# RWKV-7 chunk steps on Trainium2: one source order for all five engines, a norm in four stages, outputs in two tiles

## The chip, the core and the metric

The kernel runs on one core of a Trainium2 chip. A core has a matrix engine (TensorE, in the profile PE, with its weight loads as PEld), three elementwise engines (VectorE or DVE, ScalarE or ACT, GpSimd or POOL) and SyncE (SP), which here only issues DMAs. Each engine takes its own instructions strictly in order; across engines they wait for one another on semaphores. The metric is the device time of one execution in microseconds (us), as the median of several runs.

## What is computed

A decoder of two layers over 512 positions of width 1024 in float32: a sparse attention mixer with an MLP, then an RWKV-7 mixer with an MLP, and a last norm. The change is in the RWKV-7 mixer alone. Its core is a recurrence over the positions, for 16 heads of 64:

```
def step(state, inp):
    r_t, w_t, k_t, v_t, kk_t, b_t = inp
    sa = jnp.einsum('bhvk,bhk->bhv', state, -kk_t)
    state = (state * w_t[:, :, None, :] + sa[..., None] * b_t[:, :, None, :]
             + v_t[..., None] * k_t[:, :, None, :])
    y = jnp.einsum('bhvk,bhk->bhv', state, r_t)
    return state, y
...
y = ((y - mean) * lax.rsqrt(var + LNX_EPS) * lnx_w.astype(f32).reshape(H, N)
     + lnx_b.astype(f32).reshape(H, N))
bonus = jnp.sum(rh * kh * r_k.astype(f32), axis=-1, keepdims=True) * vh
out = (y + bonus).reshape(B, L, D).astype(h.dtype) * g
return out @ w_o
```

Here g is a gate, `sigmoid(xg @ g1) @ g2`.

## The kernel before

The recurrence runs in 8 chunks of 64 positions (NCH). Within a chunk the dependence of position on position is a triangular system, solved with matrices made beforehand; from chunk to chunk a state of 64 x 64 for each head goes on. All of it is in `rwkv()`.

**Ahead of the steps.** The v projection ("V") is a dense matmul into all 8 PSUM banks; `vcopy` brings it to the tiles VT. `vmean` and `vload(n)` take a mean over each head out of it and write the result to the operand tile sv of chunk n (POOL). The triangular matrices of all chunks are inverted in `solve`, in two halves, f = 0 for chunks 0 to 3 and f = 1 for chunks 4 to 7: 30 pairs of DVE instructions each (a product into pr, an addition into tn), a memset, a copy, then DMAs that spread the result into the tiles Mt and T11. `invert` is a generator: `run(t)` draws steps of it until their estimated time is t or more; `HOLD` (1e9) between its parts ends any draw. `until(f)` draws until half f is done.

**Operands of a chunk.** `opl(n, j)`, two halves j, makes products of the chunk's keys on PE into a PSUM tile with tag d (there are two of those), and masks them on DVE into abd (or AL) and BL. `opt(n)` transposes keys into BL. `merge1(n)` and `merge2(n)` extend the inverse from 32 x 32 blocks to 64, with a copy sa between and copies into Mt behind; `acopy(n)` moves a part by eight DMAs.

**A step** of chunk n: `step_z` (PE) and its copies Zb; `step_u` (PE) and four copies into sv; `step_s` and `step_n` (PE), which end in the product of the new state on DVE, in sv of the next chunk; `step_r` and `step_y` (PE) give the output y of the chunk, copied on ACT. The next `step_z` needs the new state. Then `gnorm(n)`: square (ACT), sum over a head (DVE), Sqrt (ACT), a reciprocal square root refined in four small DVE instructions, the product with it (DVE), the product with lnw (POOL), the addition of the bonus bv (POOL); `turn(n)` transposes y on PE into yT. `out(f)` takes yT of four chunks, adds a bias and multiplies by the gate gT (the tile ot, DVE), and splits it into a high part oh (ACT) and a low part ol (DVE or POOL). `wo(f)` is the output projection of that half, eight blocks m of 24 matmuls; its weights come as wraw by DMA and are split in two by ACT (L93) and DVE (L101). gT comes from `g2`, eight blocks of four matmuls.

**What sets the order.** Outside a block marked `manual_schedule` a scheduler places each engine's instructions by priority. Before, only PE was in such a block, and only in the loop over the steps: PE's order there was the source's, three pieces of a step with pieces of operands, merges, g2 (`G2P`) and wo(0) (`WOP`) drawn in between by `fill()`. DVE, ACT, POOL and SP were placed by the scheduler.

Of the kernel before, what the change touches and what calls it, by code (L numbers as in the profile page):

```python
# [10 lines left out]
OP = mybir.AluOpType  # L11
# [754 lines left out]
def rwkv(c, x, ks, gi):  # L766
# [348 lines left out]
    def merge(n):  # L1115
        mt = Mt[n // 4][:, :, n % 4]
        t11 = T11[n // 4]
        with c.hp("merge"):
            sa = merge1(mt, t11, n)
        yield  # L1120
        with c.hp("merge"):
            merge2(mt, sa)
        yield

    def merge1(mt, t11, n):
# [9 lines left out]
    def merge2(mt, sa):  # L1135
# [57 lines left out]
    def opt(n):  # L1193
# [4 lines left out]
        for i in range(2):  # L1198
            cp(TE[i], BL[n][E2[1 - i], 1, :, 64:128], pt[E2[i], :, 1])
# [40 lines left out]
    @c.site("g2")  # L1240
    def g2m(m, ah, al, bh):
# [375 lines left out]
```

## Time and profile before

| | us |
|---|---|
| median of 3 runs (1373.76 to 1376.73) | 1375.86 |
| the profiled execution | 1374.03 |
| its span on the core | 1372.2 |
| start: V's end to z of step 1 | 816.6 to 855.5 |
| six step periods: z of step 1 to z of step 7 | 855.5 to 960.3 |
| tail: z of step 7 to the start of wo(1), about | 960.3 to 982.0 |

Times within the span count from its start. A step period is told from one z to the next. PEclk is the clock that was granted to PE: 1.00 is 2.4 GHz and 0.50 is 1.2 GHz. A row such as "[4.17 <-DVE tn L1026]" says that the engine had stood for 4.17 us, and that an instruction of DVE at line 1026 on the tile tn ended the wait.

### The profile page before, as it was taken

The numbers are of one execution on the slowest core, as the hardware profiler recorded it, in microseconds if no ns is written. First come the engines' busy times: TensorE is split into PE (matmuls) and PEld (weight loads), VectorE is DVE, ScalarE is ACT, GpSimd is POOL, SyncE is SP. The second block draws the span as 40 slices with busy tenths as digits, with TensorE's granted clock in tenths as the row PEclk, the third lists the DMA queues.
The fourth block names the chain that finished last, engine by engine and source line by source line (L and its number), as shares of the span: only waits on it lengthen the run. The fifth ranks groups of instructions, "written<-read, shape, count | busy, mean of one in ns | idle before, by whom it ended". The sixth has DMA issues, their size and how long they took to land.

```text
span 1372.2 us, 20054 instructions
## 1 busy us (share of the span) xinstructions
PE 1295.9 (94%) x8197; PEld 1065.6 (78%) x8197; DVE 800.8 (58%) x1429; ACT 593.6 (43%) x1005; POOL 171.3 (12%) x168
## 2 busy tenths in 40 slices
PE   7989899999999999999999896877999999999997
PEld 6767566888888888898578674667988888888887
DVE  5689974553431445339888888577865532245422
ACT  5545693343311434228776332655543421134421
POOL 0386750000000000000000011334220000000000
PEclk9999999999999999999999895989999999999998
DMA  7100013221323224303302414433532222322401
GB/s 287 62 31 32 1 69 117 100 93 62 123 92 123 80 74 153 123 32 123 123 31 53 128 52 98 74 95 132 185 105 80 92 92 94 122 92 83 162 1 62
DMA packets 68283, 128.04 MB, mean 93 GB/s; under 512 B 32864, under 2 KB 39648, under 8 KB 67424
## 3 DMA queue, kind: packets, MB, share of 16 engines
q1 hardware_dynamic: 65952, 124.53, 27.7%
q10 hardware_dynamic: 2240, 2.24, 0.5%
q8 instruction: 64, 1.05, 0.3%
q14 instruction: 27, 0.22, 0.0%
HBM read 115.74 MB, written 6.82 MB: 89 GB/s over the span
## 4 chain that ended last, share of the span: by engine, by line
PE 80%; DVE 12%; issue 3%; ACT 2%; POOL 2%; DMA 1%; SPq 0%; ACTq 0%; DVEq 0%; POOLq 0%
PE g L119 20%; PE g L120 20%; PE g L121 20%; PE g L628 2%; PE d L613 1%; DVE rot L411 1%; DVE w L101 1%; DVE L L587 1%; DVE pr L1025 1%; DVE tn L1026 1%; POOL kl L99 1%; DVE acc L497 1%; PE g L1308 1%; PE g L993 1%; PE g L1324 1%
## 5 line engine op out<-in xcount | busy, mean ns | idle before, releaser
L101 DVE TENSOR_TENSOR w<-wraw,w 128x1024 fp32r<-128x1024 f32 x189 | 232.8, 1255 | 109.4 <-ACT w L93 109.1
L93 ACT ACTIVATE w<-wraw 128x1024 fp32r<-128x1024 f32 x198 | 201.2, 1048 | 139.9 <-DMA wraw<-in_wblk 106.9
L119 PE MATMUL g<-sh,w 128*128 128x512 f32 (+1 forms) x608 | 216.5, 356 | 0.0
L120 PE MATMUL g<-sl,w 128*128 128x512 f32 (+1 forms) x608 | 216.1, 355 | 0.0
L121 PE MATMUL g<-sh,w 128*128 128x512 f32 (+1 forms) x608 | 216.1, 355 | 0.0
L120 PE MATMUL g<-al,w 128*128 128x512 f32 x512 | 200.0, 391 | 0.2 <-DVE al L257 0.2
L119 PE MATMUL g<-ah,w 128*128 128x512 f32 x512 | 200.1, 391 | 0.0
L121 PE MATMUL g<-ah,w 128*128 128x512 f32 x512 | 199.9, 390 | 0.0
L273 ACT ACTIVATE sh<-r 128x512 fp32r<-128x512 f32 x64 | 40.4, 631 | 227.2 <-DVE r L271 227.2
L119 PEld LDWEIGHTS g<-sh,w 128*128 128x128 f32 x608 | 114.9, 189 | 16.4
L121 PEld LDWEIGHTS g<-sh,w 128*128 128x128 f32 x608 | 114.9, 189 | 16.3
L120 PEld LDWEIGHTS g<-sl,w 128*128 128x128 f32 x608 | 114.9, 189 | 16.2
L119 PEld LDWEIGHTS g<-ah,w 128*128 128x128 f32 x512 | 96.5, 189 | 20.2
L120 PEld LDWEIGHTS g<-al,w 128*128 128x128 f32 x512 | 96.4, 188 | 20.4 <-DVE al L257 0.6
L121 PEld LDWEIGHTS g<-ah,w 128*128 128x128 f32 x512 | 96.5, 189 | 20.1
L271 DVE SCALAR_TENSOR_TENSOR r<-g,rstd 128x512 f32<-128x512 f32 x64 | 44.1, 691 | 97.0 <-PE g L121 84.6
L275 DVE TENSOR_TENSOR sl<-q,sh 128x512 fp32r<-128x512 f32 x64 | 44.4, 693 | 75.1 <-ACT q L274 75.1
L295 DVE TENSOR_TENSOR x<-g,x 128x512 f32<-128x512 f32 x26 | 18.0, 691 | 107.4 <-PE g L121 107.4
L179 ACT ACTIVATE sq<-x 128x256 f32<-128x256 f32 (+1 forms) x56 | 26.7, 499 | 105.1 <-DVE x L295 56.4
L922 POOL MEMSET seg<- 128x512 f32 x1 | 0.5, 528 | 487.2 <-DVE xl L101 487.2
L597 ACT ACTIVATE L<-L,st 128x256 f32<-128x256 f32 (+3 forms) x64 | 35.1, 553 | 14.0 <-DVE st L595 13.9
L274 ACT ACTIVATE q<-r 128x512 f32<-128x512 f32 x64 | 39.4, 615 | 0.0
(310 smaller groups left out, 2458.6 us busy)
## 6 DMA issues: line engine op xcount, KB each, us to landing
wraw<-in_wblk SPq DMA_DIRECT2D x98, 1024.0 KB, 4.8
wraw<-in_wblk SPq DMA_DIRECT2D x5, 512.0 KB, 5.6
x<-in_xT SPq DMA_DIRECT2D x8, 256.0 KB, 5.1
x<-in_xT SPq DMA_DIRECT2D x2, 1024.0 KB, 6.5
xs<-x SPq DMA_DIRECT2D x2, 1024.0 KB, 4.9
abd<-AR SPq DMA_DIRECT2D x64, 32.0 KB, 1.9
vb<-VT SPq DMA_DIRECT2D x16, 128.0 KB, 3.8
x<-xs SPq DMA_DIRECT2D x2, 1024.0 KB, 5.1
```

What stands on the lines that cost most here:

```text
L93: s.wsp = s.nc.scalar.activation(hi, r, AF.Copy)
L101: s.nc.vector.tensor_sub(out, a, b)
L119: s.nc.tensor.matmul(p, whi[:, kc, :], ahi, start=first and kc == 0, stop=False)
L120: s.nc.tensor.matmul(p, whi[:, kc, :], alo, start=False, stop=False)
L121: s.nc.tensor.matmul(p, wlo[:, kc, :], ahi, start=False, stop=last and kc == KC - 1)
L179: nc.scalar.activation(sq, xk, AF.Square)
L271: nc.vector.scalar_tensor_tensor(r, p, 0.0, rstd, op0=OP.max, op1=OP.mult)
L273: nc.scalar.activation(hi, r, AF.Square)
L274: nc.scalar.activation(q, r, AF.Square)
L275: nc.vector.tensor_sub(lo, q, hi.bitcast(F32))
L597: nc.scalar.activation(L[g][:, :n], L[g][:, :n], AF.Exp, bias=nmx[:, g:g + 1], scale=0.125, accum_out=sm[:, g:g + 1])
L628: nc.tensor.matmul(po[HF[e]], v[sc // 2][:, j:j + 64], st8[tb, pr, e][:, sc], start=sc == 0, stop=sc == tb)
```

## The change

One block now sets the order of PE, ACT, DVE, SP and POOL together, from the copies of V to the end of the last step, and the engines' instructions in it stand as the source has them. The source order is written out anew. All eight blocks of g2 stand ahead of the steps, and all eight blocks of wo(0) behind them (four stood within them). The norm is in four stages gA (square), gB (sum), gC (Sqrt) and gD (the rest), which tables place one to three steps behind their chunk. The outputs of four chunks share a tile (two tiles in all). The bonus is taken straight from VT by two POOL instructions on 64 partitions each, so the tiles VB and their 16 DMAs go, and `bo` is one DVE copy where it was four. The copies of merges are all ACT's, two of four having been DVE's. The memsets of bd and sv stand earlier. Weights for wo(0) are fetched from behind the loop on.

```
-    bo = c.tmp.tile([128, NCH, 8], F32, name="bo", tag="bo", bufs=1)
-    for b in range(2):
-        for s in range(2):
-            nc.vector.tensor_copy(bo[E2[b], s::2].rearrange("p n (a e) -> p n a e", e=2), pbo[E2[s], :, :, b])
+    bo = c.tmp.tile([128, 64], F32, name="bo", tag="bo", bufs=1)
+    nc.vector.tensor_copy(bo, pb[:, 0, :64])
...
-        for b in range(2):
-            nc.sync.dma_start(VB[n][E2[b]].rearrange("p (a j) -> p a j", a=4), v4[:, :, b])
...
+    def gD(n, eng=nc.gpsimd):
+        sq, st = gs.pop(n)
+        m, sd, y, u, o = (st[:, i] for i in range(5))
+        nc.vector.reciprocal(y, sd)
+        nc.vector.tensor_mul(u, m, y)
+        nc.vector.scalar_tensor_tensor(u, u, -0.5, y, op0=OP.mult, op1=OP.mult)
+        nc.vector.scalar_tensor_tensor(o, u, 1.5, y, op0=OP.add, op1=OP.mult)
+        y3 = g3(YY[n])
+        nc.vector.tensor_tensor(y3, y3, o[:, :, None].to_broadcast([128, 8, 64]), op=OP.mult)
+        bv = c.t("bv")
...
+        for b in range(2):
+            nc.gpsimd.tensor_tensor(bv[E2[b]].rearrange("p (a e i) -> p a e i", a=4, e=2), v4[:, :, b],
+                                    bs[:, :, b, :, None].to_broadcast([64, 4, 2, 64]), op=OP.mult)
         eng.tensor_tensor(y3, y3, lnw, op=OP.mult)
+        eng.tensor_tensor(YY[n], YY[n], bv, op=OP.add)
...
-    until(0)
+    with c.tc.manual_schedule(engines=set(MAN)):
+        run(9e8)
+        run(1)
+        run(1)
+        for i in VL[:3]:
+            vcopy(i)
+        vmean(0)
+        vload(0)
+        opn(1, 0)
+        for i in VL[3:]:
+            vcopy(i)
+        del ps
+        opn(1, 1)
...
+        g2(0)
+        g2(1)
+        opt(1, (0, 0))
+        g2(2)
+        g2(3)
+        step_z(0)
+        for m in range(4, 8):
+            g2(m)
+        vload(1)
+        run(RUN1)
+        merge2(0, merge1(0))
+        for n in range(NCH):
+            more = n < NCH - 1
+            if n:
+                step_z(n)
...
+            if n and more:
+                acopy(n + 1)
+                opn(n + 1, 0)
+                vload(n + 1)
+            for k in GB.get(n, ()):
+                gB(k)
+            if n < 3:
+                run(RUN2)
+            step_u(n)
+            if more and n != 3:
+                sa[n + 1] = merge1(n + 1)
+            for k in GB.get(n, ()):
+                gC(k)
+            if more:
+                pn = step_s(n)
+                step_n(n, pn)
+            py = step_r(n)
+            if more:
+                sbd(n)
+            step_y(n, py)
+            for k in GB.get(n, ()):
+                gD(k)
...
+            if n and more:
+                opn(n + 1, 1)
+            if n == 3:
+                sa[4] = merge1(4)
+            if more:
+                merge2(n + 1, sa[n + 1])
+            if n and n < NCH - 2:
+                opt(n + 1, (0, 0) if n < 3 else TE)
+            for k in TU.get(n, ()):
+                turn(k)
+            for k in GA.get(n, ()):
+                gA(k)
+    c.prefetch(PFA)
+    out(0)
+    gB(6)
+    gC(6)
+    gD(6)
+    gA(7)
...
+    gD(7, nc.vector)
     w0 = wo(0)
...
+    turn(5)
+    turn(6)
+    for _ in w0:
+        pass
+    turn(7)
     out(1)
...
+GA = {2: (0,), 3: (1, 2), 4: (3,), 5: (4,), 6: (5,), 7: (6,)}
+GB = {3: (0,), 4: (1, 2), 5: (3,), 6: (4,), 7: (5,)}
+TU = {4: (0,), 5: (1, 2), 6: (3,), 7: (4,)}
```

Three places show what that does to the engines' rows. The first is DVE after V. Lines 1025 and 1026 are the inverse (its first half has the tile tn_6101 before and tn_6098 in the change, its second half tn_6099 in the change); vm is the mean, and d, kon to abd and BL are the masks of chunk 1. Before:

```order
L1025 TENSOR_TENSOR pr_6139<-tn_6101 128x198
L1273 TENSOR_REDUCE vm_6442<-VT_6431 128x16
L1026 TENSOR_TENSOR tn_6101<-tn_6101,pr_6139 128x9x22
L1274 TENSOR_SCALAR vm_6442<-vm_6442 128x16
L1273 TENSOR_REDUCE vm_6442<-VT_6431 128x16
L1025 TENSOR_TENSOR pr_6139<-tn_6101 128x184
L1274 TENSOR_SCALAR vm_6442<-vm_6442 128x16
L1273 TENSOR_REDUCE vm_6442<-VT_6432 128x16
L1026 TENSOR_TENSOR tn_6101<-tn_6101,pr_6139 128x8x23
L1179 TENSOR_TENSOR abd_5987<-d_6459,kon_2262 64x4x64
L1025 TENSOR_TENSOR pr_6139<-tn_6101 128x168
L1179 TENSOR_TENSOR abd_5987<-d_6459,kon_2262 64x4x64
```

Now, the last rows of the second half and what follows (the 62 rows of that half stand together, right behind the last of the first half):

```order
L1026 TENSOR_TENSOR tn_6099<-tn_6099,pr_6401 128x2x29
L1025 TENSOR_TENSOR pr_6401<-tn_6099 128x30
L1026 TENSOR_TENSOR tn_6099<-tn_6099,pr_6401 128x30
L1028 MEMSET tn_6099 128x32
L1029 COPY tn_6099<-tn_6099 128x1024
L1245 TENSOR_REDUCE vm_6431<-VT_6428 128x16
L1246 TENSOR_SCALAR vm_6431<-vm_6431 128x16
L1171 TENSOR_TENSOR abd_5984<-d_6503,kon_2262 64x4x64
L1171 TENSOR_TENSOR BL_6502<-d_6503,kon_2262 128x4x64 x2
L1171 TENSOR_TENSOR abd_5984<-d_6529,kon_2262 64x4x64
L1171 TENSOR_TENSOR BL_6502<-d_6529,kon_2262 128x4x64 x2
L1290 TENSOR_TENSOR sv_6430<-g_6712,pc_5323 64x512
```

The mean and the masks stood among the first half's last rows; now both halves of the inverse are ahead of them. The second place is PE at the same point, from the last rows of opl(1) on. Before (L1244 to L1247 g2, L1196 opt, L1129 merge1, L1308 z):

```order
L1185 MATMUL d_6487<-AR_5061,KB_5867 64x64
L1244 MATMUL g_6444<-sg_5351,w_6340 128x512
...
L1244 MATMUL g_6480<-sg_5351,w_6340 128x512
L1196 MATMUL d_6508<-ident_75,KB_5360 128x128 x2
...
L1129 MATMUL g_6524<-T11_6367,Mt_5421 32x32
L1244 MATMUL g_6544<-sg_5351,w_6340 128x512
...
L1139 MATMUL g_6551<-Mt_5421,sa_6541 32x32
L1308 MATMUL g_6577<-sv_6441,abd_5987 64x64 x3
```

Now (L1176 opl, with d_6503 its first half and d_6529 its second; L1233 g2, L1188 opt, L1260 z, L1119 merge1):

```order
L1177 MATMUL d_6503<-AR_5059,KB_5526 64x64
L1176 MATMUL d_6529<-AR_5060,KB_5702 64x128 [waits DVE_49,PE_49]
...
L1233 MATMUL g_6551<-sg_5351,w_6337 128x512
...
L1188 MATMUL d_6565<-ident_75,KB_5360 128x128 x2
...
L1260 MATMUL g_6591<-sv_6430,abd_5984 64x64 x16
...
L1119 MATMUL g_6640<-T11_6364,Mt_5421 32x32 x8
```

The second half of opl(1) now waits for a DVE instruction, the last mask of the first half, whose PSUM tile it takes over; g2, opt and z stand behind it. The third place is behind the last step, on PE and POOL. PE before, around the end of step 7 (L1354 y, L1396 turn, w and oh or ol a block of wo(0)):

```order
L121 MATMUL g_8240<-oh_7854,w_7502 128x256
L1354 MATMUL g_8184<-sv_6441,BL_7921 64x64 x16
L1396 MATMUL g_8287<-ident_75,y_7834 128x128 x4
...
L119 MATMUL g_8353<-oh_7854,w_8155 128x256
L1396 MATMUL g_8401<-ident_75,y_8114 128x128 x4
```

PE now (L1310 y, L1363 turn of chunks 4, 5 and 6):

```order
L1310 MATMUL g_8021<-sv_6430,BL_7818 64x64 x16
L1363 MATMUL g_8058<-ident_75,y_7492 128x128 x4
L1363 MATMUL g_8147<-ident_75,y_7492 128x128 x4
L1363 MATMUL g_8153<-ident_75,y_7492 128x128 x4
L119 MATMUL g_8163<-oh_8084,w_8070 128x256
L120 MATMUL g_8163<-ol_8085,w_8070 128x256
```

wo(0) had begun ahead of y of step 7; now its first row is behind the turn of chunk 6. POOL's last rows of the mixer before (L1383 is the product with lnw, L1387 the addition of bv, L99 an ol):

```order
L99 TENSOR_TENSOR ol_7855<-ot_7876,oh_7854 128x256
L99 TENSOR_TENSOR ol_7855<-ot_7884,oh_7854 128x256
L1386 TENSOR_TENSOR bv_8040<-vb_7416,bo_5973 128x512
L1383 TENSOR_TENSOR y_7834<-y_7834,lnw_6520 128x512
L1387 TENSOR_TENSOR y_7834<-y_7834,bv_8040 128x512
L1386 TENSOR_TENSOR bv_8237<-vb_7645,bo_5973 128x512
```

And now (L1353 lnw, L1354 the addition, L1351 bv):

```order
L1353 TENSOR_TENSOR y_7492<-y_7492,lnw_6792 128x512
L99 TENSOR_TENSOR ol_8085<-ot_8090,oh_8084 128x256
L1351 TENSOR_TENSOR bv_8126<-VT_6429,bo_5973 64x512 x2
L99 TENSOR_TENSOR ol_8085<-ot_8098,oh_8084 128x256
L1354 TENSOR_TENSOR y_7492<-y_7492,bv_8126 128x512
L1351 TENSOR_TENSOR bv_8142<-VT_6429,bo_5973 64x512 x2
L99 TENSOR_TENSOR ol_8085<-ot_8106,oh_8084 128x256
L99 TENSOR_TENSOR ol_8085<-ot_8114,oh_8084 128x256
```

The four ol of POOL stood ahead of the norms of the last three chunks; now they stand among the operations of chunks 6 and 7.

## Rows read from the trace of the kernel before

**Rows 1.** The page: busy tenths and granted clock in 40 slices.

```profile
PE   7989899999999999999999896877999999999997
PEclk9999999999999999999999895989999999999998
```

**Rows 2.** Stretches: start:end length, busy PE, PEld, DVE, ACT, POOL, clock, DMA share.

```profile
834.20:855.50 21.30, 16.66 (x248) 13.76 (x250) 19.02 (x52) 6.01 (x13) 0.00 (x0) 0.50 0.49 100
...
884.30:898.10 13.80, 11.15 (x273) 9.36 (x274) 7.66 (x17) 9.00 (x19) 4.29 (x5) 1.00 0.13 21
898.10:913.90 15.80, 14.11 (x273) 12.16 (x273) 8.98 (x19) 7.08 (x15) 5.35 (x6) 0.78 0.52 134
...
855.50:960.30 104.80, 85.77 (x1716) 73.02 (x1712) 68.64 (x147) 59.61 (x118) 39.77 (x35) 0.92 0.39 99
...
870.80:873.00 2.20, 2.20 (x18) 1.54 (x12) 1.07 (x3) 0.37 (x1) 1.26 (x1) 1.00 0.23 37
954.40:960.30 5.90, 5.90 (x52) 5.77 (x50) 3.24 (x10) 4.49 (x8) 0.44 (x1) 1.00 0.54 181
```

**Rows 3.** Timeline of PE: start, length, engine, line, operation, [idle before <-releaser].

```profile
848.71 0.70 PE L1324 MATMUL g<-bd,Mt 128*64 128x128 f32 x4 [4.17 <-DVE tn L1026]
...
855.52 0.47 PE L1308 MATMUL g<-sv,abd 128*64 128x64 f32 x3
...
960.29 0.39 PE L1308 MATMUL g<-sv,abd 128*64 128x64 f32 x6
```

**Rows 4.** Timeline of DVE at the end of wo(0).

```profile
981.98 0.48 DVE L1404 SCALAR_TENSOR_TENSOR ot<-yT,vec,gT 128x256 f32<-128x256 f32 x1
982.37 0.42 DVE L1424 TENSOR_TENSOR x<-g,x 128x256 f32<-128x256 f32 x1
```

**Rows 5.** PE's waits, 816 to 985 us: total, times, longest.

```profile
PE g L1308 <- DVE sv L1346: 7.8, 7, 3.8
PE g L1139 <- ACT sa L1113: 6.5, 4, 4.9
```

**Rows 6.** Timeline of DVE at the mean and the second inverse.

```profile
813.82 1.22 DVE L1273 TENSOR_REDUCE vm<-VT 128x16 f32<-128x1024 f32 x1 [3.27 <-ACT VT L1223]
...
828.82 0.20 DVE L1025 TENSOR_TENSOR pr<-tn 128x30 f32<-128x30 f32 x1
...
845.38 0.36 DVE L1026 TENSOR_TENSOR tn<-tn,pr 128x198 f32<-128x198 f32 x1
...
847.51 0.84 DVE L1111 COPY Mt<-g 32x256 f32<-32x256 f32 x2
...
851.52 1.05 DVE L1029 COPY tn<-tn 128x1024 f32<-128x1024 f32 x1
```

**Rows 7.** Groups, 810 to 985 us: shapes, count, busy, mean ns, idle before.

```profile
L1179 DVE TENSOR_TENSOR abd<-d,kon 64x256 f32<-64x256 f32 x28 | 11.8, 422 | 14.9 <-PE d L1185 14.4
L1179 DVE TENSOR_TENSOR BL<-d,kon 128x256 f32<-128x256 f32 x28 | 10.5, 405 | 0.0
...
L1357 ACT ACTIVATE y<-g 128x512 f32<-128x512 f32 x8 | 4.7, 590 | 0.4 <-PE g L1354 0.4
...
L1383 POOL TENSOR_TENSOR y<-y,lnw 128x512 f32<-128x512 f32 x7 | 8.9, 1274 | 23.1 <-DVE y L1381 23.1
L99 POOL TENSOR_TENSOR ol<-ot,oh 128x256 fp32r<-128x256 f32 x4 | 3.4, 864 | 3.8 <-ACT oh L104 3.8
```

**Rows 8.** Timelines of DVE and of POOL around step 7.

```profile
957.82 1.23 DVE L101 TENSOR_TENSOR w<-wraw,w 128x1024 fp32r<-128x1024 f32 x1 [0.84 <-ACT w L93]
...
961.13 2.24 DVE L101 TENSOR_TENSOR w<-wraw,w 128x1024 fp32r<-128x1024 f32 x1
...
952.56 1.27 POOL L1387 TENSOR_TENSOR y<-y,bv 128x512 f32<-128x512 f32 x1
953.79 1.04 POOL L1386 TENSOR_TENSOR bv<-vb,bo 128x512 f32<-128x512 f32 x1
...
962.37 2.14 POOL L1387 TENSOR_TENSOR y<-y,bv 128x512 f32<-128x512 f32 x1
```

More of the change, by code (lines that the diff above doesn't have):

```diff
@@ L1113, in cp, with merge1 @@
             nc.scalar.activation(out, a, AF.Copy)
[L1115 to L1125, printed above, removed]
+    @c.site("merge")
+    def merge1(n):
+        mt, t11 = Mt[n // 4][:, :, n % 4], T11[n // 4]
         pa = c.bank("g", (128, 8, 64))[:, :, :32]
@@ L1133, in merge1, with merge2 @@
         return sa
-    def merge2(mt, sa):
+    @c.site("merge")
+    def merge2(n, sa):
+        mt = Mt[n // 4][:, :, n % 4]
         pm = c.bank("g", (128, 8, 64))[:, :, :32]
@@ L1192, in opt @@
     @c.site("opt")
-    def opt(n):
+    def opt(n, te=TE):
         pt = c.bank2((128, 8, 2, 64))
@@ L1346, in step_n, with step_r, sbd @@
             nc.vector.tensor_mul(SV[n + 1][E2[e], e], pn[E2[e]], pcb[E2[e]].to_broadcast([64, 8, 64]))
+    @c.site("step_r")
+    def step_r(n):
+        py = c.bank("g", (128, 4, 2, 64))
+        if n:
+            for q in range(8):
+                nc.tensor.matmul(py[E2[q % 2], q // 2].rearrange("p a b -> p (a b)"), sl(AR, n, q)[:, 1],
+                                 Sb[:, q].rearrange("p a b -> p (a b)"), start=q < 2, stop=False, skip_group_check=True)
+        return py
+    @c.site("step_r")
+    def sbd(n):
         for e in range(2):
@@ new lines, in gA, with gB, gC @@
+    @c.site("gnorm")
+    def gA(n):
+        sq = c.t("sq")
+        nc.scalar.activation(sq, YY[n], AF.Square, scale=0.125)
+        gs[n] = sq, c.tmp.tile([128, 5, 8], F32, name="gst", tag="gst", bufs=2)
+    @c.site("gnorm")
+    def gB(n):
+        sq, st = gs[n]
+        nc.vector.tensor_reduce(st[:, 0], g3(sq), XS, OP.add)
+        nc.vector.tensor_scalar(st[:, 0], st[:, 0], 64e-5, None, op0=OP.add)
+    @c.site("gnorm")
+    def gC(n):
+        sq, st = gs[n]
+        nc.scalar.activation(st[:, 1], st[:, 0], AF.Sqrt)
@@ L1459, in rwkv, with opn @@
-    gnorm(NCH - 1)
-    for n in range(NCH - TD, NCH - 1):
-        turn(n)
-    pull(w0, 8)
-    turn(NCH - 1)
+    yT, o, xo, yq, sa = {}, {}, [], [], {}
+    def opn(n, j):
+        if j == 0:
+            BL[n] = c.b8("BL", F32, (128, 2, 8, 128))
+        opl(n, j)
+    with c.tc.manual_schedule(engines=set(MAN)):
[11 more added lines that the diff above has]
+        opn(1, 1)
+        (ah, al_), (bh, bl) = ((a.rearrange("p a b -> p (a b)") for a in c.wget(0)) for _ in range(2))
+        nc.scalar.activation(bh[64:96], bl[64:96].bitcast(F32), AF.Copy)
+        g2(0)
[11 more added lines that the diff above has]
+            more = n < NCH - 1
+            if n:
+                step_z(n)
+            if n % 2 and more:
+                vmean((n + 1) // 2)
+            if n == 1:
+                lnw = g3(c.t("lnw"))
+                nc.sync.dma_start(lnw, c.aps["lnw"])
+            if n and more:
[20 more added lines that the diff above has]
+                gD(k)
+            if n < 2:
+                run(RUN2)
+            elif n == 2:
+                run(9e8)
+                run(1)
+                run(1)
+            if n and more:
[10 more added lines that the diff above has]
+                gA(k)
@@ L1485 @@
 RUNW = 5000
-RUN1 = 3300
+RUN1 = 9000
+RUN2 = 2500
 XG = 2
```

146 lines of the change are left out of this document (27 added, 119 removed).

## The prediction

> **What bounds the kernel now.** I read four views. The page first: over most of the span TensorE is near full, and there the change alters nothing; only slices 24 to 28 dip, in the busy line's digits and in its granted clock [rows 1]. That is the recurrent stage, some 816 to 982 us. The table of stretches splits it [rows 2]: a **start** (816.6 to 855.5, where step 1's z matmuls begin), six step periods (855.5 to 960.3, where z of step 7 begins [rows 3]) and a **tail** up to about 982.0, where the last addition of wo(0) is at 982.37 [rows 4] and wo(1) takes over. In the periods PE is busy 85.8 of 104.8 us. So PE alone does not bound the stage; the recurrence does, in which each step goes z, copy, u, copy, n, product, next z. The third view, PE's waits, agrees: the largest kinds inside the steps are those for the state product sv on DVE, 7.8 us, and for the copy sa on ACT, 6.5 us [rows 5]. In the last view, DVE's own rows, the second inverse (62 instructions, 828.82 to 851.52) runs with little beside it, while the first inverse's final rows are shared with vmean and masks [rows 6].
>
> **The change, part by part.** I walk the new order with the old durations.
>
> *Start.* In the new DVE order all 62 rows of the second inverse precede the first vmean and the masks of chunk 1. (The block begins with one run that is meant to finish an inverse; the first is already used up by then, so it drains the second, and the later runs find nothing.) On PE the second half of opl(1) takes the PSUM slot of the first half, so it waits for those masks, and all of g2, opt(1) and z(0) are queued behind it. DVE comes free for the solve at 810.55: the 3.27 us it waited there for VT [rows 6] are no longer waited. The 17 rows of the first inverse still to come take 5.2 us (as the second's from 845.38 to 851.48, less 0.84 for two Mt copies), copy 1.05, the second inverse 851.5 - 828.8 - 0.8 = 21.8, copy 1.05: 839.7. Then vmean 1.22 and its scale 0.17, and masks of 2 x 0.42 + 2 x 0.41 [rows 6, 7]: PE goes on at **842.7**, having stood since some 817.5 (V's end at 816.6 and one half of opl), 25 us. PE's clock was at 0.50, its level of 1.2 GHz, in all of 834.2 to 855.5 [rows 2], after a like pause, so the first work is slow: opl, two g2 and opt, 4 us at full clock (two g2 take 2.0 of a 2.20 stretch [rows 2], opl and opt 1.0 each), are taken as 7. Then at full clock two g2, z(0) and four g2 to 856.4; merge1, copy, merge2 and copy, 3.2; and from u to the next z 5.5 (6.8 before, 848.71 to 855.52, at half clock [rows 3]): z(1) at **865.1**, where it was at 855.5. **+9.6.** The old trace alone gives nearly that: from 834.2 to z(1) took 21.3 us, less 4.2 of waiting for an inverse's row [rows 3], plus what is now ahead of z(1) too (half of opl, opt, five g2, 6.8): 866.6. All eight g2 are then done; four of them stood in the periods before.
>
> *Steps.* The old trace has a period without any g2 or wo block: 884.3 to 898.1, 13.8 us, PE busy 11.15, ACT 9.00, DVE 7.66, POOL 4.29 [rows 2]. The new periods do that work: 13.8 is the upper bound, and 10.3 the lower (11.15 less some 0.07 at each of 12 groups, whose last matmul's end shows as busy only because a gap follows). Behind y of a step ACT has five copies or squares of 0.6 and a pair of 0.75 in a row, each behind its PE group (y 0.59 [rows 7]); PE has opl, merge2, opt, turn and z, 4.3 us, so Zb comes about 1.0 us late and u waits for it. So 11.7 in a plain step. Step 3 adds 2.2 (the table load before the first Sqrt, and merge1(4), copy and merge2 in a row), step 4 adds 1.7 (two chunks' reductions, 2 x 0.86, ahead of the product on DVE), step 5 0.5 (two turns): 11.7 + 11.7 + 13.9 + 13.4 + 12.2 + 11.4 = **74.3** against 104.8. **-30.5**, and z(7) at 939.4. What went out of the periods: four g2 (4), three wo blocks (11.3), some 15 of waits, that is weight splits ahead of a product on DVE, Mt copies on it, and the low clock. Each norm stage is two or three steps old when read, so it hides; vb's 16 DMAs leave SP, where nothing waited for them: 0. bv is now two POOL operations of about 1.04 instead of one, and POOL's 5.8 us a step still fit: 0 in the steps.
>
> *Tail.* Four of wo(0)'s blocks lay in the old steps; now all eight stand on PE behind turn(4), (5) and (6), and turn(6) waits for the norm of chunk 6, whose square is only issued after step 7's y. Step by step: y(7) copied at 946.1, yT(4), square(6) to 947.3. Sqrt(6) stands on ACT behind yT(5), so behind POOL's y+bv(5): 951.0. Reciprocal to product on DVE, with four ot (0.48 each [rows 4]) between: 954.8. Then POOL in its order: lnw 1.27, ol 0.86, bv 2 x 1.04, ol 0.86, y+bv 1.27 [rows 7, 8]: 961.4 at the earliest. In the same time DVE does four weight splits and three ol. Such pairs got in each other's way before: a split took 1.23 alone and 2.24 beside POOL's y+bv, and that 2.14 in place of 1.27 [rows 8]. Taken as one after the other, 4.9 of splits against 6.3 of POOL, y+bv(6) is done near 966. Then turn(6), bv(7), two ol, and the first wo(0) block is done between 965.7 and 970.3, having begun at half clock after some 12 us with hardly a matmul. The other seven take 2.95 each at full clock (5.90 for two [rows 2]) and turn(7) 0.6: wo(1) starts between 989.0 and 994; I take **991.5**, nearer the middle since the POOL operation just ahead of the slowed pair kept its time. From z(7) that is 52.1, where it was 21.7: **+30.4**.
>
> The Trainium skill (SBUF — State Buffer, Who interferes with whom) says that a VectorE instruction with two SBUF inputs contends with a GpSimd instruction that reads SBUF, which speaks against putting ol, bv and the splits together here. The trace agrees as to the pair just named; by the rule alone the tail would be at its upper end, 994, and without it at 989.
>
> *Sum.* +9.6 - 30.5 + 30.4 = +9.5 on the profiled execution's 1374.03: 1383.5. The median of the runs is 1.8 above that execution, so about **1385**.
>
> **The rivals.** 1. *The steps run at PE's own work* (faster). With no wait for Zb, product or sa, six periods at the lower bound of 10.3 are 62, which is 12.3 less than I count; with the tail at its early end 2.5 more: 1385 - 14.8 = **1370**. For it: the splits and Mt copies that delayed products are gone from DVE's steps. Against it: ACT's 9.00 us of 11, in order, each operation behind a PE group. It decides from a mean period of 10.8 down, with the tail as taken (12.4 less 9.5 / 6): with more than that per step the lost cover for wo(0) is not paid back.
>
> 2. *The clock falls in the steps.* It was 0.78 in one old period, 898.1 to 913.9 [rows 2]; a gap of 1 us in each new period could do the same. A dip of 7 us costs about 3 (7 us of slow work is 3.5 of fast, and some of it hides): three make **1394**. For it: PE now never has a dense block in the periods. Against it: 884.3 to 898.1, equally without one, kept 1.00.
>
> 3. *No difference.* Periods of 10.8 with the tail as taken: **1376**, within 0.2%.
>
> 4. *The change does not do what it says*: the second inverse is spread over the steps and masks are early. Then PE resumes at 819 and z(1) is at some 845: **1365**. The order speaks against it.
>
> **How the numbers follow.** Forecast 0.50 (1379 to 1392), rival 1 0.20, rival 2 0.15, rival 3 0.10, rival 4 0.05. Faster by over 0.2% (2.75 us, about what a measurement of this kernel can tell from no change): 0.25; within: 0.10; slower: 0.65. The range goes from rival 1, 1370, less 1, to periods of 13.8 with the tail at its late end, 1385 + 8.5 + 2.5 = 1396, and leaves out rival 4 and a little at each end: 1369 to 1396.
>
> **What would show it.** Right: PE idle from about 817 to 842 with the masks as its releaser; z(1) near 865; z to z 11 to 14 us; PE nearly idle from about 946 to 960 at half clock, ended by POOL's y+bv; wo(1) near 991. Wrong: masks before 830, periods under 10.5, or a wo(0) that starts before 958.

## The result: 1.5% slower, and the profile after

The changed kernel takes 1396.93 us in the median (1393.86 to 1399.08), 1.0153 times the kernel before, with a 95% interval of 1.0130 to 1.0176. The forecast was 1385, in a range that ended at 1396: the direction was right, the size was not. The medians differ by 21 us, the profiled executions by 19.8; 9.5 were worked out.

The profiled executions differ by 1393.86 - 1374.03 = 19.8, and so do the spans. I cut both spans at the same events: the end of V, z of step 1, z of step 7, the last addition of wo(0).

| stage, us | before | after | difference | forecast |
|---|---|---|---|---|
| V's end to z(1) | 38.9 | 47.2 | +8.2 | +9.6 |
| six step periods | 104.9 | 80.5 | -24.4 | -30.5 |
| z(7) to the last addition of wo(0) | 22.1 | 53.6 | +31.5 | +30.4 |
| from there to the end | 389.9 | 394.7 | +4.8 | 0 |

V itself ends 0.3 earlier (816.1), so the sum is +19.8. Two lines are off by much: the steps by 6, and the part behind wo(0), which had no term.

The page of the changed kernel, in its lines of the span, PE's busy tenths and the granted clock; they answer to [rows 1].

```profile
span 1392.1 us, 20052 instructions
PE   8988899999999999999998947883899999999997
PEclk9999999999999999999998988997899999999999
```

The dip of slice 24 (a 4 now) is the pause ahead of the masks, that of slice 28 (a 3) the pause ahead of wo(0). Slices 26 and 27, which lie in the steps, stand at 8 and 8, where 8 and 7 stood.

The table of stretches of the changed kernel, with the columns of [rows 2]: the pause, the six periods, z(7) to the first matmul of wo(0), most of wo(0), the start of wo(1).

```profile
816.20:842.70 26.50, 1.55 (x49) 1.33 (x50) 23.70 (x68) 3.61 (x6) 1.99 (x2) 0.62 0.39 86
...
863.30:943.80 80.50, 67.96 (x1622) 57.03 (x1617) 46.11 (x103) 51.73 (x108) 34.32 (x31) 0.96 0.19 45
...
943.80:971.70 27.90, 6.89 (x110) 5.84 (x109) 20.79 (x40) 13.77 (x29) 19.71 (x13) 0.71 0.61 226
971.70:994.30 22.60, 22.60 (x176) 22.60 (x174) 8.09 (x12) 6.28 (x7) 3.27 (x4) 0.91 0.14 47
994.30:1010.00 15.70, 10.86 (x74) 10.45 (x73) 11.57 (x24) 7.63 (x14) 0.00 (x0) 0.78 0.45 154
```

PE has 1.55 us of work in the first 26.5 and 6.9 in the 27.9 ahead of wo(0), and in both the granted clock falls. Who is waited for stands in PE's waits from 815 to 1012 us of the changed kernel, which answer to [rows 5]:

```profile
PE d L1176 <- DVE BL L1171: 25.0, 1, 25.0
PE g L1363 <- POOL y L1354: 19.3, 2, 16.2
PE g L1268 <- ACT bd L1262: 11.9, 7, 2.5
PE g L120 <- DVE ol L101: 4.5, 1, 4.5
PE g L1131 <- ACT sa L1111: 1.3, 4, 0.5
PE g L1260 <- DVE abd L1171: 1.2, 1, 1.2
```

In order: the masks behind both inverses (the 25 us forecast), turn(6) and, for 3.1 us, turn(5) behind POOL's norm, u behind Zb in all seven steps, and wo(1) behind the low parts of out(1). The last two rows are short: merge2 behind the copy sa, and z(5) behind its masks. The old waits are gone: for sa 1.3 where 6.5 stood [rows 5], for the product on DVE no row at all.

**The steps.** The six periods took 11.45, 11.47, 13.68, 16.10, 15.87 and 11.94, against a forecast of 11.7, 11.7, 13.9, 13.4, 12.2 and 11.4. Steps 4 and 5 alone are off by more than 0.6. DVE at the end of step 4 and the start of step 5, where z(5) begins at 916.00, in the changed kernel:

```profile
911.02 1.41 DVE L1290 TENSOR_TENSOR sv<-g,pc 64x512 f32<-64x512 f32 x2 [5.77 <-PE g L1286]
912.47 0.20 DVE L1341 RECIPROCAL gst<-gst 128x8 f32<-128x8 f32 x1
...
914.35 1.13 DVE L1343 SCALAR_TENSOR_TENSOR gst<-gst 128x8 f32<-128x8 f32 x1
...
915.72 1.66 DVE L1346 TENSOR_TENSOR y<-y,gst 128x512 f32<-128x512 f32 x1
917.40 0.88 DVE L1171 TENSOR_TENSOR abd<-d,kon 64x256 f32<-64x256 f32 x2
```

And ACT and POOL at the same place:

```profile
919.69 0.59 ACT L1111 ACTIVATE BL<-d 64x512 f32<-64x512 f32 x1 [3.43 <-DVE BL L1109]
...
921.47 1.19 ACT L1262 ACTIVATE bd<-g 64x512 f32<-64x512 f32 x2
...
914.17 1.29 POOL L1353 TENSOR_TENSOR y<-y,lnw 128x512 f32<-128x512 f32 x1 [10.04 <-DVE gst L1341]
```

Two chunks' gD, the last stage of a norm, stand here on DVE for 4.9 us, in front of the last masks that z(5) reads. The first takes 1.45 us; the second, beside POOL's product and addition for the first, takes the rest. z(5)'s second half waits 1.2 for the masks. DVE's BL copy comes behind them, ACT's BL copy behind that one, then the copy of a turn and a square, and then Zb: u(5) waits 2.5.

**The tail.** POOL of the changed kernel, the lnw product of chunk 5 and of chunk 6:

```profile
943.00 1.28 POOL L1353 TENSOR_TENSOR y<-y,lnw 128x512 f32<-128x512 f32 x1 [6.15 <-DVE y L1346]
...
958.22 6.53 POOL L1353 TENSOR_TENSOR y<-y,lnw 128x512 f32<-128x512 f32 x1 [4.19 <-DVE y L1346]
```

DVE beside the second of them:

```profile
957.99 4.62 DVE L101 TENSOR_TENSOR w<-wraw,w 128x1024 fp32r<-128x1024 f32 x4
...
962.53 1.09 DVE L101 TENSOR_TENSOR ol<-ot,oh 128x256 fp32r<-128x256 f32 x3
```

The same product takes 1.28 alone and 6.53 beside four weight splits and three low parts ol; it ends 1.1 us after the last of these. The splits, at 1.15 each, are no slower than the 1.23 of one alone [rows 8]. PE where wo(0) begins, at turn(7) and where wo(1) begins:

```profile
970.92 1.12 PE L1363 MATMUL g<-ident,y 128*128 128x128 f32 x4 [16.18 <-POOL y L1354]
...
993.91 0.60 PE L1363 MATMUL g<-ident,y 128*128 128x128 f32 x4
...
1002.84 0.58 PE L120 MATMUL g<-ol,w 128*128 128x256 f32 x1 [4.52 <-DVE ol L101]
```

And DVE's low parts of out(1):

```profile
1002.37 2.77 DVE L101 TENSOR_TENSOR ol<-ot,oh 128x256 fp32r<-128x256 f32 x8
```

The wait of 4.52 is most of the part that had no term. In the source turn(7) stands behind all eight blocks of wo(0). The tail lies outside the `manual_schedule` block, and the scheduler put turn(7) behind seven of the eight (993.91). out(1) needs turn(7)'s copy, and its eight ot and eight low parts stand on DVE among four weight splits, so DVE gets to the low parts only at 1002.37. The first addition of wo(1) comes 10.2 us behind the last of wo(0) (997.39); before it came 4.5 behind (982.37 [rows 4]). DVE before and after:

```profile
986.90 0.42 DVE L1424 TENSOR_TENSOR x<-g,x 128x256 f32<-128x256 f32 x1 [0.60 <-PE g L121]
...
1007.57 0.42 DVE L1391 TENSOR_TENSOR x<-g,x 128x256 f32<-128x256 f32 x1 [2.43 <-PE g L121]
```

### The profile page after: what moved, and what is told of

Its sections match the earlier page's. It is cut to its first block, busy times and chain, and to the rows that moved or that the text cites. A ratio compares the mean times of both kernels' runs of the same rounds, so it can differ in the third digit from the quotient of the medians.

```text
span 1392.1 us, 20052 instructions
## 1 busy us (share of the span) xinstructions
PE 1287.2 (92%) x8197; PEld 1060.3 (76%) x8197; DVE 790.3 (57%) x1407; ACT 601.2 (43%) x1024; POOL 183.8 (13%) x176
## 3 DMA queue, kind: packets, MB, share of 16 engines
q1 hardware_dynamic: 61600, 122.44, 26.5%
## 4 chain that ended last, share of the span: by engine, by line
PE 81%; DVE 11%; ACT 3%; POOL 2%; issue 2%; DMA 0%; ACTq 0%; DVEq 0%; POOLq 0%
PE g L119 20%; PE g L120 20%; PE g L121 20%; PE g L628 2%; DVE w L101 1%; DVE tn L1026 1%; DVE pr L1025 1%; PE d L613 1%; DVE rot L411 1%; DVE L L587 1%; PE g L1268 1%; POOL kl L99 1%; PE g L993 1%; DVE acc L497 1%; ACT bd L1262 1%
## 5 line engine op out<-in xcount | busy, mean ns | idle before, releaser
L101 DVE TENSOR_TENSOR w<-wraw,w 128x1024 fp32r<-128x1024 f32 x189 | 229.0, 1237 | 108.7 <-ACT w L93 108.6
L119 PEld LDWEIGHTS g<-sh,w 128*128 128x128 f32 x608 | 114.9, 189 | 16.2
L120 PE MATMUL g<-ol,w 128*128 128x256 f32 x128 | 37.9, 297 | 4.5 <-DVE ol L101 4.5
L1176 PE MATMUL d<-AR,KB 64*64 64x128 f32 x256 | 18.7, 285 | 25.0 <-DVE BL L1171 25.0
```

What stands on the lines that cost most here:

```text
L101: s.nc.vector.tensor_sub(out, a, b)
L119: s.nc.tensor.matmul(p, whi[:, kc, :], ahi, start=first and kc == 0, stop=False)
L120: s.nc.tensor.matmul(p, whi[:, kc, :], alo, start=False, stop=False)
L1176: nc.tensor.matmul(pl[E2[1 - e], e, q].rearrange("p a t -> p (a t)"), k[:, 1], ar.rearrange("p a t -> p (a t)"), start=True, stop=True)
```

## The experiments

All ratios are to the kernel before, run on the same chip at the same time; the changed kernel's is 1.0153. Stages are cut as in the table above. V's end moved between 816 and 822 from run to run, in code that no edit touches, so a stage is read by its own length.

**The drain at the start.** Edit:

```
-        run(9e8)
-        run(1)
-        run(1)
```

> Edit: the three draws of the inverse at the head of the block are taken out, so the second inverse is drawn by the later runs, 50 of its 62 rows behind the masks of chunk 1 and ahead of the first state product. Theory (the drain ahead of the masks costs the start): the changed kernel stands 25.0 us on PE for these masks; here that wait is under 3 us, the solve lies beside g2, z(0), u and n, z of step 1 comes at 838 to 845 instead of 863.3, and the time falls by 18 to 23 us, to 1374 to 1379. Rival (the solve has to be done somewhere ahead of step 4, and DVE's product waits for it): the wait only moves to the first product or to merge1(4), z of step 4 comes less than 8 us earlier, and the time falls by under 8 us.

Measured: 1.0091 (1.0073 to 1.0109), 0.6% less than the change, between what the theory and its rival gave. V's end to z(1) fell from 47.2 to 37.3, by 9.9; everything behind kept its length. ACT's longest wait in that run:

```profile
830.77 0.60 ACT L1215 ACTIVATE VT<-d 128x512 f32<-128x512 f32 x1 [13.51 <-DMA dt<-tn]
```

PE's two long ones there:

```profile
826.39 0.44 PE L1176 MATMUL d<-AR,KB 64*64 64x128 f32 x1 [6.31 <-DVE pr L1025]
834.46 0.79 PE L1236 MATMUL g<-sg,w 96*128 96x512 f32 x1 [4.51 <-ACT w L1411]
```

The drain is the cause of the wait of 25 us, but to take it out gives back less than half of it. A wait of 6.3 for the first inverse's rows takes its place. ACT, in order, stands 13.5 us at a copy of V that waits for the DMA which reads tn, so g2's weights come late and PE waits another 4.5; and PE's clock was 0.50 from 829 to 838 and 0.55 from 848.7 to 856.3. The start is then 1.6 shorter than before the change.

**Turns and squares behind the next z.** turn(k) and gA(k) move from the end of a step to behind the z of the next, so that Zb passes them on ACT:

```
+        def late(n):
+            for k in TU.get(n, ()):
+                turn(k)
+            for k in GA.get(n, ()):
+                gA(k)
...
             if n:
                 step_z(n)
+                late(n - 1)
...
-            for k in TU.get(n, ()):
-                turn(k)
-            for k in GA.get(n, ()):
-                gA(k)
+    late(NCH - 1)
```

> Edit: the turns and the squares of the norm stand behind the next step's z and its two copies Zb instead of ahead of them, on PE and ACT. Theory (ACT's queue delays Zb): u waited for Zb in all seven steps, 11.9 us in total, 0.9 to 2.5 each; here these waits are under 0.5 each, periods are 10.5 to 11.2 where plain, and the time falls by 5 to 10 us, to 1387 to 1392. Rival (ACT's work is only moved: four copies of u or sa then wait behind it): the waits turn up at s, n or merge2, the periods stay within 0.5 of 11.45, 11.47, 13.7, 15.5, 15.9 and 11.9, and the time changes by under 3 us.

Measured: 1.0079 (1.0062 to 1.0096), 0.7% or 10 us less than the change. PE's waits, with the lines that changed most:

```profile
PE g L1363 <- POOL y L1354: 15.7, 2, 10.4
PE g L1268 <- ACT bd L1262: 4.9, 5, 1.2
```

The wait for Zb went from 11.9 to 4.9, and the periods from 80.5 to 73.5: the turns' copies and the squares, queued ahead of Zb on ACT, were the price in steps 3 to 6. Steps 1 and 2, which had neither there, kept 11.45 and 11.47 and their waits of 0.9 and 1.0, behind ACT's copies of BL and Mt; under 0.5 was expected. The tail fell by 3.1 too, and POOL says why:

```profile
951.77 1.27 POOL L1353 TENSOR_TENSOR y<-y,lnw 128x512 f32<-128x512 f32 x1
```

This is lnw of chunk 6. Here it runs ahead of the splits, and takes 1.27 where it took 6.53.

**gD between the masks and the transposed keys.** Edit: `gD(k)` moves from behind `step_y` to behind `opn(n + 1, 1)`.

> Edit: gD, the last stage of a norm, stands behind the masks of opl(n+1, 1) instead of ahead of them on DVE. Theory (in step 4 two gD, one instruction of which took 1.13 in place of 0.17 and one 1.66 in place of 0.69 beside POOL, hold back the masks, and z(5) for them): z(5), 3.02 us long in the changed kernel, takes 1.15, that period falls from 15.5 by 2 to 3, others by under 0.5, and the time falls by 2 to 4 us, to 1393 to 1395. Rival (the period is long for its low clock alone, 0.78): z(5) is short but the periods stay, and the time changes by under 1 us.

Measured: 1.0181 (1.0157 to 1.0205), 0.3% more than the change, where less was expected. The wait of z(5) is gone, but PE's next one is longer:

```profile
924.67 1.98 PE L1268 MATMUL g<-bd,Mt 128*64 128x128 f32 x16 [5.98 <-ACT bd L1262]
```

gD now delays DVE's BL copy, ACT's copy waits for that one, and Zb stands behind it. Step 5 got 3.1 longer (18.94), in part by the clock: it was 0.82 there, 1.00 in the changed kernel, and u took 1.98 for its 16 matmuls, 1.09 at full clock.

**gD behind the transposed keys too.** Edit: the same two lines, behind `opt(n + 1, ...)`.

> Edit: gD stands behind the masks of opl(n+1, 1) and behind the copies of opt(n+1), where e6_masks_first had it between the two. Theory (e6_masks_first lost since the copy of opt on DVE was left behind two gD, ACT's copy of the same tile waited for it, and Zb stood behind that on ACT: u(5) waited 5.98): here z(5) is 1.15 to 1.3 long and u(5) waits under 2.5, periods 4 and 5 are 2 to 5 us shorter together than the changed kernel's 32.0, and the time falls by 2 to 5 us. Rival (DVE's order is not what makes those periods long, their low clock or POOL is): both waits go, the periods stay within 1 us, and the time stays within 1 us.

Measured: 1.0167 (1.0152 to 1.0182), not to be told from the change. Steps 4 and 5 together took 27.9 instead of 32.0, but step 6 took 14.7 instead of 11.9: u(6) waited 3.15 for Zb instead of 1.91, and the clock was 0.88 where it had been 1.00. So a part of the wait went one step on, and a dip of the clock came with it. The 2.5 us of step 5 (15.87 to 13.35, both at 1.00) are this order's; step 4's share (14.56, at 0.88) is the clock's, as the rows under "What step 4 cost" show.

**The norm of chunk 6 off POOL.** Its last two operations go to DVE:

```
-    gD(6)
+    gD(6, nc.vector)
```

> Edit: the product with lnw and the addition of bv of chunk 6 go to DVE instead of POOL. Theory (POOL is held up by DVE's weight splits, on the path to turn(6)): POOL's product of 1.28 took 6.53 us beside four splits, and turn(6) waited 16.2 us for POOL; here turn(6) comes at 962 to 966 instead of 971.7, wo(0) starts some 5 us earlier, and the time falls by 4 to 7 us, to 1390 to 1393. Rival (not POOL but the whole tail is late: wo(0) waits for ol and weights next): the wait of turn(6) falls, but wo(0)'s first block waits for ol on POOL or DVE instead, and the time falls by under 2 us.

Measured: 1.0147 (1.0121 to 1.0172), not to be told from the change, though the tail is 3.1 shorter (50.5). POOL in that run:

```profile
962.95 3.89 POOL L1351 TENSOR_TENSOR bv<-VT,bo 64x512 f32<-64x512 f32 x2
```

DVE in that run:

```profile
959.93 6.00 DVE L101 TENSOR_TENSOR w<-wraw,w 128x1024 fp32r<-128x1024 f32 x4
```

The held lnw is gone, but turn(6) still waits 13.3. bv remains on POOL and takes 3.89 instead of 2.18, and now the splits give way too (1.50 each). So most of this wait is the chain of chunk 6 itself. To free the held product was worth 3.1 us; what the contention that is left costs was not tried.

**turn(5) and turn(6) inside wo(0).** Edit: in the source they stand behind the first and the third block instead of ahead of all. In the trace each stands one block earlier, turn(5) behind the first matmul of the first block and turn(6) at 987.32, behind two blocks.

> Edit: of the changed kernel's tail only PE's order: turn(5) behind the first block of wo(0), turn(6) behind the third; the operands stay where they are. Theory (POOL's queue, held up by DVE, is what is late, and wo(0)'s first block needs its ol too): PE does wait for ol on POOL, the last of which ended at 975.1, instead of for turn(6), and the time falls by under 3 us. Rival (it is the turn ahead of the blocks on PE that holds them): wo(0) starts at 963 to 966, some 7 earlier, and the time falls by 5 to 8 us.

Measured: 1.0160 (1.0131 to 1.0189), no gain; the tail took 54.0. PE's waits of that run, for the operands of wo(0):

```profile
PE g L119 <- ACT oh L104: 7.8, 1, 7.8
PE g L120 <- POOL ol L99: 6.7, 3, 3.1
PE g L120 <- DVE ol L101: 4.0, 2, 2.2
```

With turn(6) out of the way, wo(0) waits for oh and for POOL's ol instead. These stand among the norms on ACT and POOL, so PE's order was not what held it.

**Operands of wo(0) early.** `out(0)` moves into step 7, and blocks of wo(0) go between the turns:

```
+            if n == NCH - 1:
+                out(0)
             py = step_r(n)
...
+    next(w0)
+    next(w0)
     gB(6)
     gC(6)
-    gD(6)
+    gD(6, nc.vector)
+    turn(5)
+    next(w0)
...
```

> Edit: out(0), the operands of wo(0), is issued inside step 7, behind u's copies; behind the loop two blocks of wo(0) come first, then the norm of chunk 6 (its last two operations on DVE), turn(5), a block, the norm of chunk 7, turn(6), two blocks, turn(7), the last three. Theory (the tail costs what it does because wo(0)'s operands and the turns ahead of it wait for the norms of chunks 5 and 6): in the changed kernel the first wo(0) matmul comes 27.9 us behind z(7) and the last addition 53.6; here the first comes 8 to 13 behind z(7), PE stays at full clock from there, the last addition comes 33 to 38 behind z(7), and the time falls by 15 to 22 us, to 1375 to 1382. Rival (ACT's and DVE's work of the tail, four weight splits, sixteen splits of operands and two norms, is itself the length): wo(0) starts early but waits for weights and out(1), and the time falls by under 8 us.

Measured: 1.0131 (1.0109 to 1.0154), 0.2% less than the change. The tail did not shrink (54.8). PE at its two longest waits:

```profile
962.81 0.58 PE L119 MATMUL g<-oh,w 128*128 128x256 f32 x1 [10.89 <-ACT w L93]
...
972.69 0.58 PE L121 MATMUL g<-oh,w 128*128 128x256 f32 x1 [6.29 <-DVE w L101]
```

Now the weights are late: their splits stand behind the outputs and norms on ACT and DVE. But turn(7) comes three blocks earlier here (at 986.23, behind four of the eight), out(1)'s work with it, and the part behind wo(0) falls from 394.7 to 391.0. That is 3.7 of the 4.8 that had no term.

**The weights split within the steps.** The same, with one weight fetched and split in each of steps 3 to 6:

```
+            if 3 <= n < NCH - 1:
+                c.prefetch(len(c.ready) + 1)
```

> Edit: e5_wo_early, with one weight split of wo(0) in each of the steps 3 to 6, behind the state product on DVE and behind sa on ACT. Theory (in e5_wo_early wo(0) had its operands by 957 and then stood 10.9 us for a weight on ACT and 6.3 for one on DVE, which the norms of chunks 6 and 7 preceded): here the first matmul of wo(0) comes 13 to 16 us behind z(7), PE has no wait over 3 us in the tail, wo(0)'s last addition comes 36 to 42 behind z(7) where it was 53.6 in the changed kernel, the steps lose under 3 us to the splits, and the time falls by 10 to 17 us, to 1380 to 1387. Rival (the splits cost the steps as much as they save behind them, as the kernel before had it with a product behind a split): z(1) to z(7) grows by 8 or more, and the time falls by under 6 us.

Measured: 1.0155 (1.0138 to 1.0172), no gain. The tail fell from 53.6 to 43.8, and the periods grew from 80.5 to 89.8. The steps lost what the tail gained: 4.3 of it in step 5 and 5.0 in step 6, whose clock was 0.92 and 0.70. The kernel before paid in the same place, with splits ahead of the product on DVE. How much of the 9.3 is the splits and how much the clock was not separated.

**turn(7) after four blocks of wo(0).** In the source it stands behind five blocks, in the trace behind four (988.42). Edit:

```
-    for _ in w0:
-        pass
-    turn(7)
+    for m in w0:
+        if m == 4:
+            turn(7)
```

> Edit: turn(7) stands behind the fourth of wo(0)'s eight blocks instead of behind the last. Theory (the last turn's place exposes the chain yT, ot, oh and ol, wo(1)): in the changed kernel turn(7) ends at 994.5 and PE is busy 10.9 of the 15.7 us behind it, though the norm of chunk 7 was done at 975.1 at the latest; here the chain is covered by four blocks, PE goes from wo(0) to wo(1) without a gap over 1 us, and the time falls by 5 to 8 us, to 1389 to 1392. Rival (wo(1) is late because its weights are split late, or their DMA lands late): PE still waits at the start of wo(1), now for w, and the time falls by under 2 us.

Measured: 1.0144 (1.0125 to 1.0162), not to be told from the change. The part behind wo(0) fell by 2.3, to 392.4. DVE at the start of wo(1) in that run:

```profile
997.91 2.35 DVE L101 TENSOR_TENSOR w<-wraw,w 128x1024 fp32r<-128x1024 f32 x2
...
1000.79 2.35 DVE L101 TENSOR_TENSOR w<-wraw,w 128x1024 fp32r<-128x1024 f32 x2
1003.06 2.77 DVE L101 TENSOR_TENSOR ol<-ot,oh 128x256 fp32r<-128x256 f32 x8
```

The eight ol stand behind four splits, so an earlier turn does not help them all the way: wo(1) still waits 2.2, where it waited 4.5.

**Four edits together.** The drain out, late turns, early operands, and gD between masks and keys.

> Edit: the four edits together: no draws at the head, turns and squares behind the next z, masks ahead of gD, wo(0) early. Theory (they lie in different places, so they add): 8.5 + 10 + 15 to 22 + 3, less 2.8 of the second's gain that lies in the tail: the time falls by 33 to 41 us, to 1356 to 1364, faster than the kernel before. Rival (one wait takes the place of another, the clock falls where the periods are thin): under 25 us, not faster than the kernel before by more than 5.

Measured: 1.0027 (1.0008 to 1.0045), 1.3% or 17 us less than the change. PE's waits of that run:

```profile
PE g L1268 <- ACT bd L1262: 9.9, 7, 4.7
PE g L1363 <- POOL y L1354: 9.0, 2, 7.4
PE d L1176 <- DVE pr L1025: 6.3, 1, 6.3
PE g L119 <- ACT w L93: 5.0, 2, 4.8
```

The start and step 4 kept their gains (37.2 and 11.6 us), but step 5 took 18.5 at a clock of 0.82, turn(6) still waits for POOL's y, and wo(0) for weights. New waits took the place of the old, as the rival had it.

**The order rebuilt from all of this.** The drain out; late turns; each norm one step behind its chunk, and gD last in a step; one weight split in each of steps 3 to 6; out(0) in two halves of four of its eight blocks each, in steps 6 and 7, with every low part on DVE; the last norms on DVE; turns, and out(1), among the blocks of wo(0):

```
+GA = {n: (n,) for n in range(7)}
+GB = {n: (n - 1,) for n in range(1, 8)}
+TU = {n: (n - 2,) for n in range(2, 8)}
...
+            if n == NCH - 2:
+                og = out(0)
+                next(og)
+            if n == NCH - 1:
+                next(og, None)
...
+            for k in GB.get(n, ()):
+                gD(k, nc.vector if n == NCH - 1 else nc.gpsimd)
```

> Edit: e1, e4, e9 and e11 together, and: each norm begins one step behind its chunk, so that turn(3) is done in step 6; out(0) is issued in two halves in steps 6 and 7, all its splits on DVE; the last norms' operations are on DVE; turn(6) and turn(7) and out(1) stand among wo(0)'s blocks. Theory (start, Zb, the norm's place on DVE, and weights and operands of wo(0) are the four causes, and each is met): z(1) 37 behind V's end as in e1_no_drain, periods of 10.8 to 11.8, wo(0)'s first matmul under 9 behind z(7) and its last addition 32 to 36, and the time is 1345 to 1360, faster than the kernel before. Rival (DVE and ACT, now with the solve, the norms, the splits and the operands in the same steps, become the bound): periods over 12.5, and the time is 1365 or more.

Measured: 0.9946 (0.9930 to 0.9963), 1367.13 us: 0.5% faster than the kernel before, though less than expected. The six periods took 70.8 (34 less than before), z(7) to the last addition of wo(0) 42.5 (20 more; 32 to 36 were expected), what follows 393.0 (3 more), the start 37.3. One wait in step 7 is new:

```profile
933.14 1.56 PE L1260 MATMUL g<-sv,abd 128*64 128x64 f32 x16 [5.48 <-DVE abd L1171]
```

The first half of out(0) stands on DVE ahead of the masks that z(7) reads. In the last run that half moves behind them:

> Edit: e10_rebuilt with the first half of out(0) behind the masks and the norm of step 6 on DVE instead of ahead of them. Theory (e10_rebuilt's z(7) stood 5.48 us for masks that came behind four ot and four ol of out(0) on DVE): the wait goes, at most 2 us of it come back as a later Zb(7) or a later first block of wo(0), and the time falls by 3 to 5 us against e10_rebuilt, to 1362 to 1364. Rival (wo(0)'s first block needs the second half of out(0) anyway, which is not earlier): z(7) is earlier, wo(0) waits for oh and ol instead, and the time stays within 1.5 us of 1367.

Measured: 0.9951 (0.9933 to 0.9970), the same as the run above. The 5.48 is gone, and PE shows in its place, at u(7):

```profile
939.29 1.98 PE L1268 MATMUL g<-bd,Mt 128*64 128x128 f32 x16 [9.39 <-ACT bd L1262]
```

Zb now stands on ACT behind four oh, each of which waits for an ot on DVE.

**What step 4 cost.** Steps 4 and 5 are the same code in the change and in some of the runs, yet their lengths differ. The changed kernel's two periods in the table of stretches:

```profile
899.90:916.00 16.10, 13.77 (x274) 11.38 (x273) 8.35 (x21) 9.04 (x20) 5.85 (x6) 0.79 0.12 19
916.00:931.87 15.87, 11.95 (x279) 10.06 (x278) 12.66 (x26) 8.84 (x19) 12.07 (x11) 1.00 0.30 85
```

The same two where chunk 6's norm is on DVE, an edit that lies behind both:

```profile
902.43:915.65 13.22, 10.89 (x274) 9.32 (x273) 8.19 (x21) 9.03 (x20) 5.67 (x6) 1.00 0.14 24
915.65:933.10 17.45, 13.94 (x279) 11.52 (x278) 12.82 (x26) 8.83 (x19) 12.27 (x11) 0.80 0.28 77
```

Each has one stretch at the lower level of the clock, the one in step 4, the other in step 5. At 1.00 step 4 takes 13.2, at 0.79 it takes 16.1. So 2.9 us of it are the clock. Step 5 loses 1.6 in the same way (15.87 to 17.45); why less than step 4 was not tried.

## Why the prediction was right or wrong, point by point

The profiled execution rose by 10.3 us more than forecast: 6.1 in the steps, 4.8 behind wo(0), 1.1 in the tail, less 1.4 at the start and 0.3 by V's end.

**The start: right.** PE stood 25.0 us, with the masks as releaser, and went on at 842.2 (842.7 forecast). z(1) came at 863.3 instead of 865.1, for the most part because the clock came back sooner than taken: the first work, taken as 7 us, took 5.6, and the clock was 0.94 in the mean from 844.1 to 863.3. The run without the drain shows that its removal gives 9.9 of the 25; rival 4, which had z(1) at 845 for an inverse spread out, was too hopeful by some 9 (37.3 from V's end, not 28.4).

**The steps: right in kind, 6.2 short in size (80.5 for 74.3).** The four periods of steps 1, 2, 3 and 6 came within 0.6 each. The sum failed in two terms. The first is step 5, 12.2 forecast and 15.87 measured at full clock: +3.7. The step that failed reads "each norm stage is two or three steps old when read, so it hides". What gD reads is old, and gD never waits. But gD stands on DVE ahead of masks that z waits for, and what stands behind it was not counted: two chunks' gD are 4.9 us there. Placing it last in the step gave 2.5 of this back, and lengthened the next step by 2.8, where u waited 1.2 longer and the clock fell to 0.88. The second term is the clock in step 4, +2.9 over the 13.2 that the step takes at 1.00 (13.4 forecast). That is rival 2's mechanism, once instead of three times, at the price it named ("a dip of 7 us costs about 3"). The forecast had left it out of the sum although an old row showed such a dip. Which of the two steps the dip falls in changed from run to run, and nothing in the old trace told that it would come in step 4 here.

The term for Zb (1.0 late in a plain step) had the right mechanism and size: 0.92 and 1.02 in steps 1 and 2. The late turns took 7.0 off the wait for Zb, and 7.0 off the periods (a dip of the clock lies in either run, there in step 5).

**The tail: the right chain, and a sum that is near by a slip.** From z(7), wo(0) ended after 53.6 where 52.1 were taken. The chain was as laid out: POOL's y+bv(6) released turn(6), after a wait of 16.2 us. But the forecast's last addition does not come out of its terms. A first block done between 965.7 and 970.3, seven blocks of 2.95 and a turn of 0.6 make 987.0 to 991.6, not 989.0 to 994; the 991.5 that it took as nearer the middle is the late end. From z(7) the first block was done 2.0 later than that late end, after 32.9 instead of 30.9, so the slip hid a miss, and the nearness of the sum is in part luck.

Of the 2.0, 0.5 lie ahead of turn(6): it began 27.1 behind z(7), where the late end had 26.6. DVE's product of chunk 6 came 1.1 early, and POOL took 12.6 from lnw(6) on, where the forecast had splits and POOL one after the other, 11.2 us. Alone POOL's operations would take 6.3, and 5.3 of what they lost is in one product (6.53 for 1.27). The forecast had leaned to the middle because an old row showed the POOL operation ahead of a slowed pair keeping its time; here that operation was the one held. The other 1.5 are turn(6) and the first block at a low clock, 5.8 for 4.3. The seven other blocks and turn(7) then took 20.7, where their terms make 21.3. The Trainium skill (SBUF — State Buffer, Who interferes with whom) has VectorE and GpSimd exclude each other in such pairs, not share. The held lnw agrees with that, though it was held through seven DVE instructions and not through one.

**wo(1): the missing term, +4.8.** The change's own source has `turn(7)` and `out(1)` behind wo(0)'s last block, and the forecast let wo(1) start at wo(0)'s end. It should have walked on: turn(7), copy, eight ot, eight oh, eight ol, on a DVE that also has splits and wo(0)'s additions. The two runs whose traces have turn(7) ahead of wo(0)'s last four blocks gave 2.3 and 3.7 of it back.

**The rivals.** 1 (periods at PE's own work) fell: PE was busy 68 of 80.5 us. The rebuilt version came to a mean of 11.8 and did not reach it either. 3 fell with it. 2 held in part, as told. The range, which ended at 1396, missed by 0.9 because it had no case in which the clock's dip, the order of DVE and the start of wo(1) came together.

**What stays open.** Why the clock falls in step 4 in one run and in step 5 in another of the same code is not settled. In both, u of step 4 had stood for 2.33 us; its 16 matmuls then took 1.97 in the one and 1.09 in the other. With that wait at 1.15, in the run with late turns, step 4 took 11.6 at 1.00, and the clock fell in step 5 (0.89).

## What to carry to other kernels

When engines follow a written order, cost each moved piece by what stands behind it on its own engine, not only by whether its inputs are ready: a piece that never waits can still be the one that others wait for. Taking one wait out of such an order mostly shows the next one (25 us gave 9.9, 5.5 gave nothing), so walk the chain on past the removed wait, and past the stage that was changed, before a gain is counted. Work that was spread over a recurrence's gaps can cost more when it is gathered behind it than the gaps get shorter: here 31.5 and 4.8 us for 24.4, in the rebuilt order 20.4 and 3.1 for 34.1.

## What the runs showed of the hardware

Beside back-to-back weight splits and low parts on DVE, one POOL product was held for the whole of them: 6.53 instead of 1.28 us, while four splits kept 1.15 each. The same came in five more runs that have the two side by side (6.53 or 6.54 each time). Where POOL had an ol and bv instead, both sides lengthened: splits to 1.50 each, bv to 3.89 for 2.18. What decides between the two was not tried. DVE was held too: at the end of step 4, beside POOL's products, an instruction of 8 columns that takes 0.17 us alone took 1.13, and the product with it 1.66 instead of 0.69.
